# A hybrid encoder layer: the squares of W1 and of the input rows taken by ScalarE's accumulator instead of GpSimd sums

## The chip, the cores and the metric

One NeuronCore of a Trainium2 chip runs the whole layer in one launch. The metric is the device time of one execution in microseconds (us), lower is better. The engines are TensorE (PE; PEld is its weight load), VectorE (DVE), ScalarE (ACT), GpSimd (POOL) and SyncE (SP), which here issues every DMA of the kernel, in program order.

## The reference, cut to what matters

Input x has 2048 tokens of width 1024, all float32; there is one layer.

```python
h = rms_norm(x, norm1_g)
q, k, v, gb, gc, hin, u = split(h @ w_in)      # 3 x 512, then 4 x 256
q, k = rms_norm(q, q_norm_g), rms_norm(k, k_norm_g)          # 8 heads of 64
y_attn = chunked_band_attention(q, k, v, rel_bias)  # chunks of 64, own + 8 before
y_conv = gb * conv3(gc * hin, conv_w)
y_pool = (mean over the last 2, 4, 8, 16 tokens - u) @ pool_w * pool_scale
x = x + concat(y_attn, y_conv, y_pool) @ w_out
h2 = rms_norm(x, norm2_g)
x = x + square(relu(h2 @ w_mlp1)) @ w_mlp2     # 1024 -> 4096 -> 1024
```

The layer needs the mean square of every row of x for the first norm. The kernel's MLP runs in 16-bit halves, so it also needs a bound on the size of each column of `w_mlp1` (and of `w_mlp2`), from which it takes the powers of two that scale the operands. Finding these bounds is called the survey; it reads both weights once (64 tiles of 128x512 each) beside the attention part.

## The kernel before

Tokens are worked on in four blocks of 512 (`block(b, ...)`). Activations are held column-major: a tile of x has 128 model columns as partitions and 512 tokens along the free axis. Each block has these stages, and the order of TensorE's instructions over all of them is fixed by hand (`weave` takes attention units and fills in side work at a set rate, `InOrder` chains TensorE's instructions). The other engines and SP follow the scheduler's priorities, and each executes its own queue in order.

- **Projection.** `project(0)`, `project(1)` and `project(2)` make q, k and v, each in 8 steps over the model columns. A step loads a weight tile `rwq` (`load_w`, L137 to L143), ACT rounds it to the high part (L141), DVE subtracts to get the low part (L142), and TensorE runs 12 matmuls (three products of high and low parts for four groups of 128 tokens, L160 to L162). `project(0)` also loads the x tile (`load_x`, L392): ACT makes its high part (L395), DVE its low part (L396).
- **Row powers of x.** In `load_x` the helper `sumsq` (L203) squares the x tile on ACT and adds the square to `acc` on POOL (L209). After the eighth step `token_cols` (L211) sums `acc` over partitions with TensorE against a column of ones, in four float32 matmuls (L214) into a PSUM tile of tag "d", and DVE scales the sum (L216). `rsqrt` (an ACT square root and DVE steps) gives `rstd`. The same helpers serve the output rows (`acc2`, in `outproj`), which the change leaves alone.
- **Attention**, 32 units per block: scores (L529, L530), softmax (L533, L539), a transpose of the probabilities (L550) that ACT and DVE write as high and low part `pp` (L551, L552), values (L565). `prep` transposes k and q for the next two heads, and spreads them through DRAM and by DMA (`kd`, `kx`, `qs`, `qx`).
- **Side work**, woven between the units: the output projection of the block before (`outproj`, with `xo`, which is read, added to and stored to `x2d`), conv and pooling (`convpool`), the second norm's statistics (`stats`), and the survey.
- **Survey.** `pace` asks for one step of `survey` in two of five steps of side work. For W1 a step loads two tiles `pr` (tag "x", five buffers shared with the x tiles), ACT squares each to bfloat16 (L283), POOL adds them in three pieces (L286 to L288) into a group tile, and after eight steps TensorE sums over partitions with eight one-column matmuls (L271) that DVE copies out. For W2 a step loads two tiles `ps`, and ACT squares each with its accumulator (L300), which leaves one sum per partition. `paced` ties each square behind the latest softmax exponential on ACT.
- **Early operands.** In block 3 `early_operands` prepares the MLP input of the first tokens: it loads `er` and `e` tiles, scales them on DVE (L358), and `put` (L364, L365) writes 28 pairs of 16-bit halves, two buffers of tag "pg", each stored to DRAM (`xd`, L366).
- **MLP**, from 896 us on: Strassen-like products in 16-bit halves (L845), with all operands already scaled.

Of the kernel before, what the change touches and what calls it, by code (L numbers as in the profile page):

```python
# [8 lines left out]
F32 = mybir.dt.float32  # L9
# [9 lines left out]
P = 128  # L19
D = 1024  # L20
# [72 lines left out]
def trunk(ctx, tc, xT, cols, cinv, w_qkv, w_cp, w_out, w1, w2, nbias, pool_w, outT):  # L93
# [32 lines left out]
    ones16 = const.tile([P, 1], BF16, name="ones16")  # L126
    ve.memset(ones16, 1.0)
# [98 lines left out]
    vacc = p1.tile([P, 512], F32, name="vacc")  # L226
# [11 lines left out]
    def value_norms(k):  # L238
        raw = scr.tile([P, 512], F32, tag="x", bufs=5, name=f"vw{k}")
# [18 lines left out]
    cn = const.tile([P, FF // P], F32, name="cn")  # L258
# [8 lines left out]
    def survey():  # L267
        def norms(f0, group):
            t = pd(f"cn{f0}")
            for i in range(8):  # L270
                te.matmul(t[:, i : i + 1], group[:, i], ones16, start=True, stop=True)  # L271
            ve.tensor_copy(cn[:, f0 : f0 + 8], t[:, 0:8])

        full = None
        for ft in range(FF // P):
            if ft % 8 == 0:
                group = scr.tile([P, 8, P], BF16, tag="pg", bufs=2, name=f"pg{ft}")
            qs = []
            for half in range(2):
                raw = scr.tile([P, 512], F32, tag="x", bufs=5, name=f"pr{ft}_{half}")  # L280
                sy.dma_start(raw, w1[ft, half])
                q = scr.tile([P, 4, P], BF16, tag="pq", bufs=3, name=f"pq{ft}_{half}")
                paced(sc.activation(q.rearrange("p a b -> p (a b)"), raw, AF.Square))  # L283
                qs.append(q)
            q = qs[0]
# [3 lines left out]
            if ft % 8 == 2 and full:  # L289
                norms(*full)  # L290
            if ft % 8 == 7:
                full = (ft - 7, group)
            yield
        yield
        norms(*full)
        for i in range(64):
            raw = scr.tile([P, 512], F32, tag="x", bufs=5, name=f"ps{i}")
            sy.dma_start(raw, w2[i // 16, (i // 2) % 8, i % 2])
            q = scr.tile([P, 512], BF16, tag="pq", bufs=3, name=f"pt{i}")
            paced(sc.activation(q, raw, AF.Square, accum_out=sq2[:, i : i + 1]))  # L300
            if i % 2:
                yield

# [21 lines left out]
    def scales():  # L325
        for _ in surveyed:
            pass
        m = const.tile([P, 4], F32, name="m")
        ve.tensor_reduce(out=m[:, 0:1], in_=cn, axis=AX.X, op=ALU.max)
# [18 lines left out]
    def early_operands():  # L348
        for k in range(4):
            q = {}  # L350
            for n in range(2):
                rr = scr.tile([P, 512], F32, tag="x", bufs=5, name=f"er{k}_{n}")
                sy.dma_start(rr, r2d[n])
                for half in range(2):
                    kk = k + 4 * half
# [725 lines left out]
```

## Time and profile before

| | us |
| --- | --- |
| median of 3 runs | 2143.21 (2143.02 to 2146.45) |
| the profiled execution | 2144.97 |
| span of its trace | 2143.1 |

| engine | busy | share of the span |
| --- | --- | --- |
| TensorE | 2050.1 us | 96% |
| VectorE | 1365.9 us | 64% |
| ScalarE | 1010.9 us | 47% |
| GpSimd | 700.1 us | 33% |

The clock granted to TensorE was 0.986 of full speed on average. DMA moved 392.88 MB. A busy share is an average over stages; an idle stretch of TensorE shows in the view of waits with the engine and tile that ended it. A row of the timeline gives start, duration, engine, line, operation, tiles, and in brackets the idle time just ahead and what ended it.

### The profile page before, as it was taken

How to read it: one execution, taken by the hardware profiler on the slowest of the kernel's cores; microseconds unless marked ns; L12 is line 12 of the kernel's file. 1: busy time of each engine (PE TensorE's matmuls, PEld its weight loads, DVE VectorE, ACT ScalarE, POOL GpSimd, SP SyncE). 2: the span in 40 equal slices, each digit the busy share in tenths (PEclk: the TensorE clock that was granted, in tenths of full speed). 3: DMA queues.
4: the chain of work that ended last, by engine and by line, in shares of the span. 5: the costliest groups of instructions: out<-in, count | busy, mean ns of one | idle time of the engine just before them, and what ended most of it. 6: DMA issues, size and time to landing. Idle time of an engine off the chain costs nothing.

```text
span 2143.1 us, 31845 instructions
## 1 busy us (share of the span) xinstructions
PE 2050.1 (96%) x11136; PEld 1262.3 (59%) x11136; DVE 1365.9 (64%) x2184; ACT 1010.9 (47%) x1940; POOL 700.1 (33%) x565
## 2 busy tenths in 40 slices
PE   7999998999899699998999999999999999999999
PEld 6777787888787588864444444444444444444444
DVE  7687466856679767757768878767743053353354
ACT  5466465737665455545656446446134151150330
POOL 4254055200224213154546456445522031130132
PEclk9999999999999899999999999999999999999999
DMA  8685698549866776493465565547743333333344
GB/s 287 202 242 169 173 273 248 179 121 273 266 199 211 241 225 179 136 344 116 161 221 189 174 209 182 182 148 286 259 120 102 104 101 101 103 97 106 103 148 152
DMA packets 215824, 392.88 MB, mean 183 GB/s; under 512 B 25584, under 2 KB 32880, under 8 KB 215664
## 3 DMA queue, kind: packets, MB, share of 16 engines
q1 hardware_dynamic: 215664, 390.86, 58.2%
q8 instruction: 87, 1.43, 0.3%
q14 instruction: 73, 0.60, 0.1%
HBM read 268.60 MB, written 105.38 MB: 175 GB/s over the span
## 4 chain that ended last, share of the span: by engine, by line
PE 68%; DMA 10%; DVE 9%; issue 5%; POOL 4%; ACT 3%; SPq 1%; POOLq 0%; DVEq 0%; ACTq 0%
PE b_d L845 21%; PE b_u L845 18%; PE a L161 3%; PE a L162 3%; PE a L160 3%; PE cp L160 2%; PE o L160 2%; PE cp L161 2%; PE cp L162 2%; PE o L161 2%; PE o L162 2%; PE pt L550 2%; PE y L565 2%; DMA r_d<-w 1%; PE s L529 1%
## 5 line engine op out<-in xcount | busy, mean ns | idle before, releaser
L845 PE MATMUL b_d<-ft_u,s_d 128*128 128x512 f16 x1152 | 265.8, 381 | 7.6 <-ACT ft_u L795 3.2
L845 PEld LDWEIGHTS <-s_d 128*128 128x128 f16 x1536 | 150.5, 98 | 191.3 <-issue 10.6
L845 PEld LDWEIGHTS <-s_u 128*128 128x128 f16 x1536 | 150.6, 98 | 186.5 <-issue 7.2
L845 PE MATMUL b_u<-zt,s_u 128*128 128x512 f16 x1152 | 257.3, 381 | 1.5 <-DVE u2u L948 0.8
L966 DVE TENSOR_TENSOR acc<-acc,b_d 128x512 f32<-128x512 f32 x176 | 119.1, 682 | 179.7 <-PE b_d L845 175.4
L845 PEld LDWEIGHTS <-a_u 128*128 128x128 f16 x1152 | 112.8, 98 | 146.6 <-issue 13.5
L845 PEld LDWEIGHTS <-a_d 128*128 128x128 f16 x1152 | 112.8, 98 | 143.2 <-issue 8.4
L829 POOL TENSOR_TENSOR t1u<-u2u,c11u 128x512 f32<-128x512 f32 x32 | 43.6, 1363 | 443.5 <-ACT u2u L952 431.3
L845 PE MATMUL b_d<-fb_u,a_d 128*128 128x512 f16 x768 | 183.7, 379 | 4.0 <-DVE acc L966 1.7
L845 PE MATMUL b_u<-zb,a_u 128*128 128x512 f16 x768 | 176.6, 379 | 1.3 <-ACT u2u L935 1.3
L209 POOL TENSOR_TENSOR acc<-acc,sq 128x512 f32<-128x512 f32 x56 | 82.8, 1479 | 260.4 <-ACT sq L208 191.3
L161 PE MATMUL a<-wq,xg 128*128 128x512 f32 x384 | 155.3, 404 | 8.2 <-DVE wq L142 8.2
L160 PE MATMUL a<-wq,xg 128*128 128x512 f32 x384 | 147.4, 407 | 10.4 <-ACT wq L141 7.8
L162 PE MATMUL a<-wq,xg 128*128 128x512 f32 x384 | 154.5, 403 | 0.1
L539 ACT ACTIVATE sb<-sb,nm 128x640 f32<-128x640 f32 (+4 forms) x128 | 97.6, 762 | 115.8 <-DVE nm L533 111.5
L552 DVE SCALAR_TENSOR_TENSOR pp<-pt,pp 128x384 f16<-128x384 f32 (+1 forms) x224 | 101.8, 483 | 48.2 <-ACT pp L551 47.6
L533 DVE CUSTOM_DVE_ANT_0 sb<-s,b 128x640 f32<-128x640 f32 (+4 forms) x128 | 94.1, 735 | 52.7 <-PE s L530 51.3
L142 DVE TENSOR_TENSOR wq<-rwq,wq 128x512 fp32r<-128x512 f32 x96 | 79.9, 839 | 46.0 <-ACT wq L141 46.0
L160 PE MATMUL o<-mix,wo 128*128 128x512 f32 x256 | 106.3, 416 | 1.3 <-ACT mix L631 1.0
L160 PE MATMUL cp<-xg,wc 128*128 128x512 f32 x256 | 107.1, 418 | 0.0
L141 POOL CAST wc<-rwc 128x512 fp32r<-128x512 f32 x64 | 41.8, 653 | 195.4 <-PE cp L162 94.2
L935 ACT COPY u2u<-b_u 128x512 f32<-128x512 f32 x32 | 18.5, 578 | 179.8 <-PE b_u L845 177.5
(274 smaller groups left out, 4512.1 us busy)
## 6 DMA issues: line engine op xcount, KB each, us to landing
rwq<-w_qkv SPq DMA_DIRECT2D x96, 256.0 KB, 2.8
pr<-w SPq DMA_DIRECT2D x64, 256.0 KB, 4.8
rwc<-w_cp SPq DMA_DIRECT2D x64, 256.0 KB, 4.3
rwo<-w_out SPq DMA_DIRECT2D x64, 256.0 KB, 4.4
ps<-w SPq DMA_DIRECT2D x64, 256.0 KB, 4.5
r_u<-w SPq DMA_DIRECT2D x64, 256.0 KB, 3.4
wd<-s_u SPq DMA_DIRECT2D x64, 256.0 KB, 2.2
r_d<-w SPq DMA_DIRECT2D x64, 256.0 KB, 2.9
```

Source lines behind the costliest of these rows:

```text
L142: (lo or ve).tensor_tensor(out=w[:, 1], in0=raw, in1=w[:, 0].bitcast(F32), op=ALU.subtract)
L160: te.matmul(out, ah, bh, start=start, stop=False)
L161: te.matmul(out, ah, bl, start=False, stop=False)
L162: te.matmul(out, al, bh, start=False, stop=stop)
L209: gp.tensor_tensor(out=acc, in0=acc, in1=q, op=ALU.add)
L533: ve.tensor_tensor_reduce(out=sb[:, :nk].rearrange("p (e k) -> p e k", e=ne), in0=s[:, :ne, :hk], in1=bi[:, 640 - nk :].rearrange("p (e k) ...
L539: exps.append(sc.activation(sb[:, :nk], sb[:, :nk], AF.Exp, bias=nmx, scale=-1.0, accum_out=st["l"][:, i, j : j + 1]))
L550: te.transpose(pt[:, m * P : (m + 1) * P], sb[:, c0 + m * P : c0 + (m + 1) * P], ident)
L552: ve.scalar_tensor_tensor(out=pp[:, 1, c0:c1], in0=pt[:, :n], scalar=PSC, in1=pp[:, 0, c0:c1], op0=ALU.mult, op1=ALU.subtract)
L829: gp.tensor_tensor(out=t1, in0=b12, in1=b11, op=ALU.subtract)
L845: te.matmul(bank, w[:, a, q * P : (q + 1) * P], xs[q][:, c], start=start and q == 0 and i == 0, stop=q == n - 1 and i == 2, skip_group_che ...
L966: ve.tensor_tensor(out=a, in0=a, in1=bk, op=ALU.add)
```

## The change

- **Survey of W1.** The kernel gets a second input, `w1t`, which is W1 stored with its columns along the partitions (the host lays it out). All 128 squares of the survey are now in one loop: ACT's square with `accum_out` leaves one sum per partition, in `sq1` for W1 and `sq2` for W2. A step loads two tiles (tag "sv", four buffers) and squares the two tiles of the step before. The POOL adds, the one-column matmuls, the DVE copies and the "pq" tiles go; one DVE reduction of `sq1` is added in `scales`.
- **Row powers of x.** A third input, `xN`, is x in token-major tiles. Each step of `project(0)` also loads an `xn` tile (tag "sv"), and two steps later ACT squares it with the accumulator into `sx`. DVE reduces `sx` (`row_stats`). The POOL adds and the matmuls of this sum go; the 32 added loads are 8.4 MB.
- **Early operands.** `er` is loaded twice in all, not eight times (1.5 MB less), the four `e` tiles of a step come in one go (tag "sv"), and are worked on a step later.
- **Buffers.** Tag "x" has three buffers, not five; "sv" has four; `vacc` shares the tag "acc".

```diff
@@ sumsq, value_norms
-            q = pool.tile([P, TB + 16], F32, tag="win", bufs=2, name="sq")[:, :TB] if pool is scr else pool.tile([P, 512], F32, tag="sq", bufs=1, name="sq")
+            q = pool.tile([P, 512], F32, tag="sq", bufs=1, name="sq")
-    vacc = p1.tile([P, 512], F32, name="vacc")
+    vacc = p1.tile([P, 512], F32, tag="acc", name="vacc")
@@ survey
-            for half in range(2):
-                raw = scr.tile([P, 512], F32, tag="x", bufs=5, name=f"pr{ft}_{half}")
-                sy.dma_start(raw, w1[ft, half])
-                q = scr.tile([P, 4, P], BF16, tag="pq", bufs=3, name=f"pq{ft}_{half}")
-                paced(sc.activation(q.rearrange("p a b -> p (a b)"), raw, AF.Square))
...
-            gp.tensor_tensor(out=q, in0=q, in1=qs[1], op=ALU.add)
-            gp.tensor_tensor(out=q[:, :2], in0=q[:, :2], in1=q[:, 2:], op=ALU.add)
-            gp.tensor_tensor(out=group[:, ft % 8], in0=q[:, 0], in1=q[:, 1], op=ALU.add)
...
+        srcs = [w1t[i // 2, i % 2] for i in range(64)] + [w2[i // 16, (i // 2) % 8, i % 2] for i in range(64)]
+        held = []
+
+        def look():
+            i, raw = held.pop(0)
+            acc = (sq1, sq2)[i // 64][:, i % 64 : i % 64 + 1]
+            paced(sc.activation(raw, raw, AF.Square, accum_out=acc))
+
+        for i, src in enumerate(srcs):
+            raw = scr.tile([P, 512], F32, tag="sv", bufs=4, name=f"{'prt'[2 * (i // 64)]}{i}")
+            sy.dma_start(raw, src)
+            held.append((i, raw))
             if i % 2:
+                while len(held) > 2:
+                    look()
                 yield
@@ scales
+        ve.tensor_reduce(out=cn, in_=sq1.rearrange("p (f t) -> p f t", t=2), axis=AX.X, op=ALU.add)
@@ early_operands
-                rr = scr.tile([P, 512], F32, tag="x", bufs=5, name=f"er{k}_{n}")
-                sy.dma_start(rr, r2d[n])
...
+            for half in range(2):
+                for n in range(2):
+                    raw[half, n] = scr.tile([P, 512], F32, tag="sv", bufs=4, name=f"e{k}_{half}{n}")
+                    sy.dma_start(raw[half, n], x2d[k + 4 * half, :, n * 512 : n * 512 + 512])
+            yield
@@ block
-            xr = scr.tile([P, 512], F32, tag="x", bufs=5, name=f"x{b}_{k}")
+            xr = scr.tile([P, 512], F32, tag="x", bufs=3, name=f"x{b}_{k}")
-            sumsq(acc, xr, k == 0, scr)
+        def row_power(n):
+            raw = scr.tile([P, 512], F32, tag="sv", bufs=4, name=f"xn{b}_{n}")
+            sy.dma_start(raw, xN[4 * b + n // 2, n % 2])
+            return n, raw
+
+        def look_rows(n, raw):
+            sc.activation(raw, raw, AF.Square, accum_out=sx[:, n // 2, n % 2 : n % 2 + 1])
...
+                if c == 0:
+                    rows.append(row_power(k))
+                    if k > 1:
+                        look_rows(*rows.pop(0))
...
-        ms1 = token_cols(acc, f"ms1_{b}")
-        rstd = rsqrt(sm, ms1, NT, "r1")
+            ve.tensor_reduce(out=ms1, in_=sx, axis=AX.X, op=ALU.add)
+            ve.tensor_scalar(ms1, ms1, 1.0 / D, EPS, op0=ALU.mult, op1=ALU.add)
+            rstd.append(rsqrt(sm, ms1, NT, "r1"))
```

Three places of the instruction order follow, before and after.

Place one, block 1 with the statistics of block 0. SP's queue, from the store of `xo0_6` to the next survey loads (`pr28_1` is a tile of W1), before:

```order
L732 DMA x2d_102<-xo0_6_3902 128x512
L730 DMA xo1_0_5955<-xT 128x512
L139 DMA rwc1_0_0_4218<-w_cp 128x512
L475 DMA qs1_5_3762<-qlo1_2_3685 64x512
L470 DMA kx1_5_3760<-kd_105 128x1024
L475 DMA qs1_5_3762<-qhi1_2_3684 64x512
L475 DMA qx1_5_3763<-qhi1_2_3684 64x512
L475 DMA qx1_5_3763<-qlo1_2_3685 64x512
L481 DMA b1_5_3770<-bd_104 128x640
L281 DMA pr28_1_4188<-w1 128x512
```
The same queue after (`p54` and `p55` are tiles of `w1t`):

```order
L742 DMA x2d_100<-xo0_6_3740 128x512
L740 DMA xo1_0_5729<-xT 128x512
L137 DMA rwc1_0_0_4031<-w_cp 128x512
L485 DMA qs1_5_3611<-qlo1_2_3534 64x512
L480 DMA kx1_5_3609<-kd_103 128x1024
L485 DMA qs1_5_3611<-qhi1_2_3533 64x512
L485 DMA qx1_5_3612<-qhi1_2_3533 64x512
L485 DMA qx1_5_3612<-qlo1_2_3534 64x512
L491 DMA b1_5_3619<-bd_102 128x640
L276 DMA p54_3874<-w1t 128x512
L276 DMA p55_3876<-w1t 128x512
```
One survey load stood behind `b1_5` before, the second of its pair being issued earlier; now both loads of a pair, `p54` and `p55`, stand there. ACT's queue at the same place, before:

```order
L539 ACTIVATE sb1_4_1_4122,l1_2_4062<-sb1_4_1_4122,nm1_4_1_4123 128x640
L283 ACTIVATE pq28_0_4186<-pr28_0_4184 128x512
L283 ACTIVATE pq28_1_4190<-pr28_1_4188 128x512
L551 ACTIVATE pp1_4_0_4137<-pt1_4_0_0_4138 128x384
L551 ACTIVATE pp1_4_0_4137<-pt1_4_0_384_4144 128x256
L166 ACT_TABLE_LOAD
```
and after:

```order
L549 ACTIVATE sb1_4_1_3940,l1_2_3880<-sb1_4_1_3940,nm1_4_1_3941 128x640
L272 ACTIVATE p54_3874,sq1_116<-p54_3874 128x512
L272 ACTIVATE p55_3876,sq1_116<-p55_3876 128x512
L561 ACTIVATE pp1_4_0_3955<-pt1_4_0_0_3956 128x384
L561 ACTIVATE pp1_4_0_3955<-pt1_4_0_384_3962 128x256
L164 ACT_TABLE_LOAD
```
The two squares stand at the same place as before, between the exponential of unit 4_1 and the write of `pp1_4_0`; the table load for the square root is still behind them.

Place two, the first projection of block 0, on DVE (`xg` is the low part of x, `wq` that of the weight, `bi` a bias table), before:

```order
L142 TENSOR_TENSOR wq0_0_2_193<-rwq0_0_2_191,wq0_0_2_193 128x512
L396 SCALAR_TENSOR_TENSOR xg0_3_128<-x0_3_208,col_92,xg0_3_128 128x512
L199 TENSOR_SCALAR bi0_346<-nb0_349,col_92 128x256
L200 MEMSET bi0_346 64x64
L396 SCALAR_TENSOR_TENSOR xg0_4_129<-x0_4_232,col_92,xg0_4_129 128x512
L396 SCALAR_TENSOR_TENSOR xg0_5_130<-x0_5_256,col_92,xg0_5_130 128x512
L199 TENSOR_SCALAR bi1_354<-nb1_357,col_92 128x256
L142 TENSOR_TENSOR wq0_0_3_217<-rwq0_0_3_215,wq0_0_3_217 128x512
L200 MEMSET bi1_354 64x64
L396 SCALAR_TENSOR_TENSOR xg0_6_131<-x0_6_280,col_92,xg0_6_131 128x512
L142 TENSOR_TENSOR wq0_0_4_241<-rwq0_0_4_239,wq0_0_4_241 128x512
```
and after:

```order
L140 TENSOR_TENSOR wq0_0_2_191<-rwq0_0_2_189,wq0_0_2_191 128x512
L384 SCALAR_TENSOR_TENSOR xg0_3_126<-x0_3_206,col_92,xg0_3_126 128x512
L140 TENSOR_TENSOR wq0_0_3_215<-rwq0_0_3_213,wq0_0_3_215 128x512
L384 SCALAR_TENSOR_TENSOR xg0_4_127<-x0_4_230,col_92,xg0_4_127 128x512
L197 TENSOR_SCALAR bi0_342<-nb0_345,col_92 128x256
L140 TENSOR_TENSOR wq0_0_4_239<-rwq0_0_4_237,wq0_0_4_239 128x512
```
Before, `xg0_4`, `xg0_5` and a bias piece stood between `xg0_3` and `wq0_0_3`; now each weight follows its x tile at once.

Place three, block 3, on ACT: from the square root of k's norms (`rqs` of `ssk3`) to the high part of k (`khi3_0`), with the casts of `put` (`eb` and `et`, 28 in all) between, before:

```order
L166 ACTIVATE rqs_8558<-ssk3_8541 128x32
L141 CAST wq3_2_5_8655<-rwq3_2_5_8653 128x512
L364 CAST eb22_2_10861<-e2_11_10792 128x512
L141 CAST wq3_2_6_8681<-rwq3_2_6_8679 128x512
L364 CAST et1_2_10872<-e2_00_10687 128x512
L364 CAST et3_2_10876<-e2_01_10748 128x512
L141 CAST wq3_2_7_8722<-rwq3_2_7_8720 128x512
L364 CAST et2_2_10919<-e2_11_10792 128x512
L141 CAST wo2_0_1_8759<-rwo2_0_1_8757 128x512
L364 CAST et4_2_10923<-e2_10_10723 128x512
L141 CAST wo2_0_0_8764<-rwo2_0_0_8762 128x512
L452 CAST khi3_0_8628<-tk3_0_8623 128x512
```
and after:

```order
L353 CAST et1_2_10524<-e2_00_10332 128x512
L164 ACTIVATE rqs_8280<-ssk3_8263 128x32
L139 CAST wq3_2_6_8403<-rwq3_2_6_8401 128x512
L353 CAST et3_2_10528<-e2_01_10334 128x512
L353 CAST et2_2_10549<-e2_11_10338 128x512
L139 CAST wq3_2_7_8444<-rwq3_2_7_8442 128x512
L353 CAST et4_2_10553<-e2_10_10336 128x512
L139 CAST wo2_0_1_8481<-rwo2_0_1_8479 128x512
L353 CAST eb11_3_10653<-e3_00_10597 128x512
L139 CAST wo2_0_0_8486<-rwo2_0_0_8484 128x512
L462 CAST khi3_0_8350<-tk3_0_8345 128x512
L353 CAST eb21_3_10679<-e3_10_10601 128x512
```
`rqs` stood after `eb21_2`, and now stands two puts later, after `et1_2`; `khi3_0` stood after `et4_2`, and now stands one put later, after `eb11_3`.

## Rows read from the trace of the kernel before

**Rows 1.** The page: busy time, share of the span, instructions, by engine.

```profile
PE 2050.1 (96%) x11136; PEld 1262.3 (59%) x11136; DVE 1365.9 (64%) x2184; ACT 1010.9 (47%) x1940; POOL 700.1 (33%) x565
```

**Rows 2.** View of waits, TensorE, 0 to 900 us: total us, times, longest us.

```profile
PE s L529 <- DMA qx<-qlo: 13.0, 1, 13.0
PE a L161 <- DVE wq L142: 8.2, 6, 3.2
PE tq L448 <- DVE klo L453: 4.2, 2, 3.8
PE y L565 <- DVE pp L552: 3.8, 4, 2.2
PE tq L448 <- DVE r1r L173: 3.3, 1, 3.3
PE s L529 <- DVE nm L533: 2.3, 2, 1.7
PE a L160 <- DVE ms_3c L216: 2.3, 1, 2.3
```

**Rows 3.** Busy us by stretch: length, PE, PEld, DVE, ACT, POOL, clock, DMA share, GB/s.

```profile
411.00:431.00 20.00, 17.34 (x96) 13.85 (x95) 18.75 (x20) 14.03 (x28) 10.86 (x7) 0.91 0.67 201
...
900.00:2143.00 1243.00, 1212.04 (x5570) 561.47 (x5568) 725.89 (x894) 494.86 (x826) 444.87 (x303) 1.00 0.50 163
```

**Rows 4.** Timeline, block 0, first projection: start us, us, engine, line, operation, tiles.

```profile
7.77 0.69 DVE L142 TENSOR_TENSOR wq<-rwq,wq 128x512 fp32r<-128x512 f32 x1 [0.41 <-ACT wq L141]
12.56 1.78 DVE L142 TENSOR_TENSOR wq<-rwq,wq 128x512 fp32r<-128x512 f32 x1
...
17.48 3.33 DVE L396 SCALAR_TENSOR_TENSOR xg<-x,col,xg 128x512 fp32r<-128x512 f32 x2
21.73 0.79 PE L161 MATMUL a<-wq,xg 128*128 128x512 f32 x1 [3.16 <-DVE wq L142]
22.75 0.63 PE L160 MATMUL a<-wq,xg 128*128 128x512 f32 x1
```

**Rows 5.** DMA view, 4 to 15 us.

```profile
DMA packets 2218, 3.64 MB, mean 331 GB/s; under 512 B 247, under 2 KB 631, under 8 KB 2218
```

**Rows 6.** Timeline of TensorE: a sum over partitions, and matmuls behind it.

```profile
332.69 1.03 PE L214 MATMUL ms<-ones,acc 128*128 128x1 f32 x8
...
333.90 0.39 PE L161 MATMUL cp<-xg,wc 128*128 128x512 f32 x1
334.13 0.39 PE L162 MATMUL cp<-xg,wc 128*128 128x512 f32 x1
```

**Rows 7.** Timeline of DVE and POOL, block 0, attention.

```profile
130.70 2.48 DVE L653 SCALAR_TENSOR_TENSOR m<-w,uh 64x512 f32<-64x512 f32 x2
131.07 1.57 POOL L286 TENSOR_TENSOR pq<-pq,pq 128x512 bf16<-128x512 bf16 x1
```

**Rows 8.** Timeline of TensorE, first projection of block 2.

```profile
419.27 0.50 PE L161 MATMUL a<-wq,xg 128*128 128x512 f32 x1 [2.66 <-DVE wq L142]
```

**Rows 9.** Groups by form, ACT, 0 to 900 us: busy us, mean ns.

```profile
L300 ACT ACTIVATION_READ_ACCUMULATOR pt<-ps 128x1 f32 x64 | 12.1, 188 | 0.0
```

**Rows 10.** Timeline of SP, block 1, around place one.

```profile
322.85 0.38 SPq L732 DMA_DIRECT2D x2d<-xo  x1
327.81 0.33 SPq L730 DMA_DIRECT2D xo<-xT  x1
```

**Rows 11.** Timeline of ACT, then of TensorE, block 1, behind place one.

```profile
339.54 0.63 ACT L283 ACTIVATE pq<-pr 128x512 bf16<-128x512 f32 x1 [6.54 <-DMA pr<-w]
...
341.19 0.77 PE L550 MATMUL pt<-ident,sb 128*128 128x128 f32 x5 [3.55 <-DVE pp L552]
```

**Rows 12.** Timeline of ACT, block 3: puts, and the root of k's norms.

```profile
662.85 0.62 ACT L364 CAST eb<-e 128x512 f16<-128x512 f32 x1 [1.62 <-DVE e L358]
...
709.53 0.23 ACT L166 ACTIVATE rqs<-ssk 128x32 f32<-128x32 f32 x1
...
723.79 0.62 ACT L364 CAST et<-e 128x512 f16<-128x512 f32 x1 [3.21 <-DMA xd<-et]
```

More of the change, by code (lines that the diff above doesn't have):

```diff
@@ L238, in value_norms @@
     def value_norms(k):
-        raw = scr.tile([P, 512], F32, tag="x", bufs=5, name=f"vw{k}")
+        raw = scr.tile([P, 512], F32, tag="x", bufs=3, name=f"vw{k}")
         sy.dma_start(raw, w_qkv[2, k])
@@ L256, in value_scale @@
         ve.tensor_scalar(vsc[:, 1:2], r, 1.0 / (1024.0 * PSC), None, op0=ALU.mult)
-    cn = const.tile([P, FF // P], F32, name="cn")
+    sq1 = const.tile([P, 64], F32, name="sq1")
     sq2 = const.tile([P, 64], F32, name="sq2")
@@ L267, in survey @@
     def survey():
[L268 to L278, printed above, removed]
-            for half in range(2):
-                raw = scr.tile([P, 512], F32, tag="x", bufs=5, name=f"pr{ft}_{half}")
-                sy.dma_start(raw, w1[ft, half])
-                q = scr.tile([P, 4, P], BF16, tag="pq", bufs=3, name=f"pq{ft}_{half}")
-                paced(sc.activation(q.rearrange("p a b -> p (a b)"), raw, AF.Square))
-                qs.append(q)
-            q = qs[0]
-            gp.tensor_tensor(out=q, in0=q, in1=qs[1], op=ALU.add)
-            gp.tensor_tensor(out=q[:, :2], in0=q[:, :2], in1=q[:, 2:], op=ALU.add)
-            gp.tensor_tensor(out=group[:, ft % 8], in0=q[:, 0], in1=q[:, 1], op=ALU.add)
[L289 to L300, printed above, removed]
+        srcs = [w1t[i // 2, i % 2] for i in range(64)] + [w2[i // 16, (i // 2) % 8, i % 2] for i in range(64)]
[8 more added lines that the diff above has]
+            held.append((i, raw))
             if i % 2:
+                while len(held) > 2:
+                    look()
                 yield
+        while held:
+            look()
     surveyed = survey()
@@ L348, in early_operands @@
     def early_operands():
-        for k in range(4):
-            q = {}
-            for n in range(2):
-                rr = scr.tile([P, 512], F32, tag="x", bufs=5, name=f"er{k}_{n}")
-                sy.dma_start(rr, r2d[n])
-                for half in range(2):
-                    kk = k + 4 * half
-                    t = scr.tile([P, 512], F32, tag="x", bufs=5, name=f"e{k}_{half}{n}")
-                    sy.dma_start(t, x2d[kk, :, n * 512 : n * 512 + 512])
-                    ve.scalar_tensor_tensor(out=t, in0=t, scalar=g2s[:, kk : kk + 1], in1=rr, op0=ALU.mult, op1=ALU.mult)
+        rr = []
+        for n in range(2):
+            t = scr.tile([P, 512], F32, tag="x", bufs=3, name=f"er{n}")
+            sy.dma_start(t, r2d[n])
+            rr.append(t)
+        for k in range(4):
+            raw, q = {}, {}
+            for half in range(2):
+                for n in range(2):
+                    raw[half, n] = scr.tile([P, 512], F32, tag="sv", bufs=4, name=f"e{k}_{half}{n}")
+                    sy.dma_start(raw[half, n], x2d[k + 4 * half, :, n * 512 : n * 512 + 512])
+            yield
+            for half in range(2):
+                for n in range(2):
+                    kk, t = k + 4 * half, raw[half, n]
+                    ve.scalar_tensor_tensor(out=t, in0=t, scalar=g2s[:, kk : kk + 1], in1=rr[n], op0=ALU.mult, op1=ALU.mult)
                     q[half, n] = t
-                    yield
+                yield
             def put(src, op):
@@ L407, in project @@
                 ac = [pd(f"a{b}_{c}_{i}", "dydt"[i]) for i in range(4)]
+            rows = []
             for k in range(KT):
```

22 lines of the change are left out of this document (14 added, 8 removed).

## The prediction

> **What bounds the kernel now.** I read the page's busy shares first, then the waits of TensorE, then the stretches, and last the timelines around each long wait. TensorE is busy 96% of the span, GpSimd 33% [rows 1]. The only time to be won is TensorE's own work and its waits. From 900 us on it is busy 1212 of 1243 us [rows 3], its instructions there are the same in both kernels, and nothing of the change reaches there: I count that part as 0. So everything happens in the attention part, and there the waits that bear on the change are few [rows 2]: one wait of 13.0 us for `qx` in block 3, six waits for the low part of a weight (8.2 us), and 15.9 us in the other five lines, all of which name DVE and none GpSimd. GpSimd is not a bound. It can matter only through DVE: a low part `wq` takes 0.69 us alone at 7.77, and 1.78 us at 12.56, where a POOL add runs [rows 4]; in block 0's attention two DVE steps take 2.48 us beside the survey's add of 1.57 us [rows 7].
>
> The page "SBUF — State Buffer" of the Trainium skill (section "Who interferes with whom") states a rule for this: a DVE instruction with two SBUF inputs shares a port with a GpSimd instruction that reads SBUF, and the later one is held for the whole of the other. The trace agrees, 0.69 against 1.78 us. By the rule alone DVE could be given back up to the POOL time that goes, and the sum would be that of the second rival below.
>
> **The change part by part.** The profiled execution took 2144.97 us, 1.9 us above its span and 1.8 above the median of 2143.21. I sum against 2145.0.
>
> *Start of block 0.* DVE works on `xg0_4` and `xg0_5` ahead of the weight that TensorE needs (3.33 us for two, [rows 4]), and TensorE waits 3.16 us. In the new order (place two) the weight follows its x tile at once and no POOL add is beside it: this wait goes. Behind it TensorE runs at the lower level of its clock for a while, 0.63 us for a matmul [rows 4]. What this costs I take from the like wait in block 2, 2.66 us [rows 8], in a stretch of 20 us with a granted clock of 0.91 [rows 3]: 20 x 0.09 = 1.8 us, part of it idle anyway, so 1.5. Against it, one 256 KB tile `xn0_0` now comes ahead of the first weight: at 331 GB/s [rows 5] a tile takes 0.79 us, so +0.8. Term: -3.2 - 1.5 + 0.8 = **-3.9** (-4.7 to 0, if another wait takes its place).
>
> *TensorE's own work.* A sum over partitions is 4 float32 matmuls, recorded as 8. From 332.69 to 333.90 stand these eight and one matmul of 0.23 us (the distance of the next two), so 0.98 us at most [rows 6]; I take 0.9. The input's four go: 3.6 us. The 32 one-column bfloat16 matmuls of the survey are not more than 0.98 / 8 = 0.12 us each by that row (3.9 us), and not below 0. They have operands of half the width, so I take 0.8, nearer the lower end. Of the 4.4 us, 0.9 stand in block 3 ahead of the long wait and are counted there. Term: **-3.5** (-6.9, with 0.98 and 0.12, to -2.7).
>
> *Block 0's attention.* With no survey adds beside it, DVE's two-input steps fall back toward 0.7 us. The waits there are those for the score minimum `nm` (2.3) and some of those for `pp` (3.8) [rows 2]: 6.1 in all. I take half, since the chain TensorE-DVE-ACT-TensorE stays. Term: **-3** (-6 to 0).
>
> *First projections of blocks 1 to 3.* Of the 8.2 us for `wq`, 3.2 are at the start and 2.7 in block 2; the other 2.3 lie in four short waits. Here DVE loses the contention of eight POOL adds, but ACT, in order, has more to do: each accumulated square adds a read of 188 ns [rows 9], 96 of them, 18.0 us over the kernel, while the count of squares is unchanged. In block 2 the last `pp` writes of the block before stand behind two of the new squares, so the low part is only some 1.5 us earlier. I take -1.2 for the short waits, -1.7 for block 2 and +0.7 for block 3, where the squares of `xn3_5` to `xn3_7` come ahead of the casts. Term: **-2.2** (-6.5, all waits and the clock loss gone, to +3).
>
> *Place one, the statistics in blocks 1 and 2.* SP waits about 4.6 us (322.85 to 327.81) to issue the next load of `xo`, which needs the store to `x2d` [rows 10]. Everything behind it in its queue is late, the survey loads too. ACT then waits 6.54 us for a survey tile, and TensorE 3.55 us for `pp` [rows 11] and 3.3 us for the square root `r1r`, which ACT has behind the tile [rows 2]. "Loads a step ahead" sounds as if it ended this. The order says no: `p54` and `p55` are issued at the same place, behind the same nine DMAs, and their squares stand ahead of `pp1_4_0` as before. Now the second of two loads is waited for, which is a tile more (0.79 us) in each of the two blocks. Term: **+1.6** (-10.6, if 3.55, 3.3 and block 2's 3.8 for `klo` [rows 2] all go, to +3 for two more tiles in each).
>
> *Block 3.* The wait for `ms_3c` (2.3 us, [rows 2]) goes with its PSUM tile. The puts pace ACT: the first at 662.85, the 21st at 723.79 [rows 12], 60.94 / 20 = 3.05 us each. The `xn` squares end sooner than the old x squares did, so I start the puts about 3 us earlier. The root of k's norms ran at 709.53 behind put 16. Behind put 18 it comes at 662.85 - 3 + 17 x 3.05 + 0.6 = 712.3, 2.8 us later. The high part of k, now behind put 22, comes at 662.85 - 3 + 21 x 3.05 + 0.6 = 724.5, about where it was. So the 13.0 us for `qx` stay, and swallow part of what was won ahead of them. Term: **-2**, with the 0.9 of the sum over partitions in it (-4 to +6, two puts late and nothing won).
>
> *Copies, reductions and buffers.* The removed DVE copies and the new reductions are a few short DVE instructions far from TensorE's chain: 0. Net DMA traffic grows by 6.8 of 393 MB, at 331 GB/s 21 us of transfer, mostly in first projections; that is covered by TensorE's work there unless the first rival below holds.
>
> Sum: -3.9 - 3.5 - 3 - 2.2 + 1.6 - 2 = -13.0. 2145.0 - 13.0 = 2132.0 for an execution like the profiled one, and 1.8 less, **2130 us**, for the median.
>
> **The rivals.**
>
> 1. *The loads of `xn` bind (slower).* A step of `project(0)` has now three loads, 3 x 0.79 = 2.4 us at the rate of the start [rows 5], against 12 matmuls of 0.23 us [rows 6], 2.8 us. In block 2 that stretch already moves 201 GB/s at a share of 0.67 [rows 3]. Eight tiles more in 22 us are 95 GB/s more, a share of 0.67 x 296 / 201 = 0.99. From there each step waits, as SP's and ACT's queues are in order. Price if every added tile is paid: 32 x 0.79 = 25 us, 2155. For it: that share. Against it: three x tiles of the next block are now loaded a block ahead, and survey loads pause there. Chance 0.16.
>
> The page "DMA: Bandwidth & Descriptors" of the Trainium skill (section "Queues, rings and completion order") states that all DMAs that SP issues go through one row of rings and are taken in ring order, so an added tile holds up every later weight. No row here separates that from plain saturation; it speaks for this rival.
>
> 2. *DVE and the statistics gain fully (faster still).* All DVE waits outside block 3's long one shorten, and the loads a step ahead do end ACT's waits at place one. Then place one gives -10.6 and not +1.6 (2118), with the other terms as they are. For it: every one of these waits names DVE or ACT work that the change lightens. Against it: place one's order. Chance 0.15.
>
> 3. *No change to speak of: the change does not do what it says for TensorE.* The DVE waits of block 0 and of the first projections come from the chain of dependences, not from POOL, and block 3 pays a put. Left are start, own work and place one, -5.8, and +2 of block 3: 2145.0 - 3.8 - 1.8 = 2139. For it: the `pp` waits hang on ACT's cast too. Against it: the stretched steps [rows 4, 7]. Chance 0.15.
>
> **How the numbers follow.** The forecast (2122 to 2138) has 0.54, the rivals 0.16, 0.15 and 0.15. A measurement of this kernel can tell about 0.2% from no change, 4.3 us, so 2138.9 is the edge. Faster: 0.54 + 0.15 and 0.03 of the third rival, 0.72. Slower: nearly all of the first, 0.15. Same: 0.13. The range goes from 2115, a little below the second rival, to 2147, which takes in the third and leaves out most of the first.
>
> **What would show it.** In the trace after: no wait of TensorE near 18 us, and a first matmul at about 8.5; no POOL instruction between block 0's projections and its output sums but the value norms and the pooling windows; low parts of about 0.7 us in first projections; ACT still waiting 6 to 8 us for `p54` or `p55` near 330 and for `t106` near 565; the wait for `qx` still 10 to 15 us. The forecast is wrong if first projections show TensorE waiting for `rwq` or ACT for `xn` (first rival), or if ACT's wait at place one is gone (second).

## The result

The changed kernel takes 2132.47 us (median of four runs, 2131.75 to 2134.14), the kernel before 2143.11 us beside it; the ratio is 0.995, with a 95% interval of 0.9933 to 0.9967. Timed again in five rounds it was 0.9944 (0.9926 to 0.9962). The forecast was 2130 us, in a range of 2115 to 2147. The size is right; several of its terms are not, and that they cancel is luck.

TensorE's busy time fell by 10.1 us, GpSimd's by 121 us. The page's busy line, after, answers to [rows 1]:

```profile
PE 2040.0 (96%) x11072; PEld 1255.2 (59%) x11072; DVE 1339.8 (63%) x2184; ACT 1019.6 (48%) x2036; POOL 579.0 (27%) x441
```
TensorE's waits of the attention part, after (total us, times, longest us; the lines that bear on the change), answer to [rows 2]:

```profile
PE s L539 <- DMA qs<-qlo: 14.9, 2, 12.7
PE a L158 <- ACT wq L139: 12.5, 3, 8.4
PE tq L458 <- DVE klo L463: 10.0, 4, 3.8
PE y L575 <- DVE pp L562: 7.8, 6, 1.6
PE pt L560 <- DVE pp L562: 7.3, 8, 2.2
PE a L159 <- DVE wq L140: 1.8, 1, 1.8
PE tk L458 <- DVE nk L445: 1.7, 1, 1.7
PE s L539 <- DVE nm L543: 0.8, 1, 0.8
```
One line of the same view of before is not in [rows 2]:

```profile
PE pt L550 <- DVE pp L552: 5.8, 3, 3.5
```
The six waits for a low part `wq` are down from 8.2 to 1.8 us, those for `nm` from 2.3 to 0.8, and the wait for `ms_3c` is gone. The wait for `r1r` has only changed its name: the same matmul, at 345.85 us before and 337.68 after, now waits 3.77 us for `klo`. New is ACT's `wq`: of its 12.5 us, 8.4 are the start of the first matmul (7.8 before), and 4.1 are two waits for a high part at changes of block. `pp` costs 15.1 us in 14 waits, where it was 9.6 in seven. The wait of block 3 is 12.7 us, where it was 13.0.

One profile is not enough to place 10 us here. Both kernels were profiled again, and I compare the start of the same TensorE matmul in each profile with its start in the first profile of before (positive: earlier, in us):

```
matmul at, in the first profile    before,   changed kernel   steps
of before                          2nd       1st  2nd  3rd    moved
block 0, end of projection   84     0.0      4.4  4.6  3.7     4.8
block 0, attention          160    -0.4      5.2  5.1  3.8     5.4
block 1, projection done    235     0.1      4.0  6.2  1.6     5.0
block 1, attention begun    257     0.7      7.3  7.0  3.1     6.1
block 1, before its stats   331     0.7      6.9  6.2  1.3     0.9
block 1, behind its stats   350     1.2      7.5  6.1  1.3     8.9
block 2, projection done    475     2.8     11.0  9.3  4.8    10.2
block 2, before its stats   566     3.6      8.2  9.9  4.4     5.2
block 2, late               640     4.9      7.4 11.9  3.6    11.5
block 3, projection 0       654     4.9      4.3 10.0  0.9     9.1
block 3, end                896     4.1      8.0 14.5  4.1    13.3
MLP                        2100     3.7     13.1 15.2  7.1    15.9
```

(The third profile of the changed kernel is that of experiment 9, `steps moved` that of experiment 10.) The attention part of one and the same kernel ends 4 us apart in two profiles of before, and 10 us apart in three of the changed kernel. On average over the profiles the changed kernel leads before by 6.8 us at 896 us and by 10.0 at 2100: about 7 us come from the attention part, where the forecast had 13, and 3 from the MLP, where it had 0. The MLP, whose instructions are the same, gave -0.4 in the second profile of before and +5.1, +0.7 and +3.0 in those of the changed kernel. The 5.1 us of the first are mostly one wait near 1041 us and what follows it: 2.17 us in the first profile of before, 1.81 in the second, 0.74 in the first of the changed kernel, with matmuls at the lower clock behind it only in the first (nine take 3.79 us, and 2.10 in the others). TensorE's timeline, the first profile of before, then its second, then the changed kernel:

```profile
1041.66 3.79 PE L845 MATMUL b_d<-ft_u,s_d 128*128 128x512 f16 x9 [2.17 <-ACT ft_u L795]
```
```profile
1037.27 2.10 PE L845 MATMUL b_d<-ft_u,s_d 128*128 128x512 f16 x9 [1.81 <-ACT ft_u L795]
```
```profile
1031.94 2.10 PE L855 MATMUL b_d<-ft_u,s_d 128*128 128x512 f16 x9 [0.74 <-ACT ft_u L805]
```
The lower clock is the first profile's of before alone. The shorter wait is not scatter: it is 0.5 to 1.0 us in all twelve profiles of kernels with the change or a part of it, and 1.8 or more in both of before. ACT waits there for POOL, and POOL for a weight tile `r_d` (4.50 and 4.17 us in the two profiles of before, 2.98 in the first of the changed kernel). Why that tile lands sooner is open; it is worth about 1 us. The rest of the MLP I count as scatter, and judge what follows by medians of timed runs first, and by the traces where a mechanism is to be seen.

### The profile page after: what moved, and what is told of

Same layout as the page of the kernel before. It is cut to its first block, busy times and chain, and to the rows that moved or that the text cites. A ratio compares the mean times of both kernels' runs of the same rounds, so it can differ in the third digit from the quotient of the medians.

```text
span 2130.1 us, 31726 instructions
## 1 busy us (share of the span) xinstructions
PE 2040.0 (96%) x11072; PEld 1255.2 (59%) x11072; DVE 1339.8 (63%) x2184; ACT 1019.6 (48%) x2036; POOL 579.0 (27%) x441
## 4 chain that ended last, share of the span: by engine, by line
PE 38%; DVE 5%; POOL 3%; DMA 3%; issue 3%; ACT 2%; SPq 0%; POOLq 0%; DVEq 0%; ACTq 0%
PE b_d L855 21%; PE b_u L855 17%; DMA r_d<-w 1%; DVE ft_u L806 1%; POOL t1u L839 1%; DVE a_d L809 1%; DVE acc L976 1%; DVE s_d L809 1%; POOL r_d L824 0%; DVE x L869 0%; POOL s_d L822 0%; DVE a_u L809 0%; DMA rr<-r2d 0%; DMA xd<-yb 0%; ACT ft_u L805 0%
## 5 line engine op out<-in xcount | busy, mean ns | idle before, releaser
L855 PEld LDWEIGHTS <-a_u 128*128 128x128 f16 x1152 | 112.7, 98 | 146.3 <-issue 12.7
L158 PE MATMUL a<-wq,xg 128*128 128x512 f32 x384 | 144.6, 403 | 12.5 <-ACT wq L139 12.5
L207 POOL TENSOR_TENSOR acc<-acc,sq 128x512 f32<-128x512 f32 x28 | 38.0, 1357 | 379.2 <-ACT sq L206 353.0
L158 PE MATMUL cp<-xg,wc 128*128 128x512 f32 x256 | 106.7, 417 | 0.0
L159 PE MATMUL cp<-xg,wc 128*128 128x512 f32 x256 | 101.5, 397 | 0.0
```

Of the source, the lines that this page charges most:

```text
L158: te.matmul(out, ah, bh, start=start, stop=False)
L159: te.matmul(out, ah, bl, start=False, stop=False)
L855: te.matmul(bank, w[:, a, q * P : (q + 1) * P], xs[q][:, c], start=start and q == 0 and i == 0, stop=q == n - 1 and i == 2, skip_group_che ...
```

## The experiments

Ratios are to the kernel before, timed on the same chip, with their 95% intervals; the changed kernel has 0.995 and 0.9944.

**1. The survey alone.** The row powers of x as before:

```diff
+            sumsq(acc, xr, k == 0, scr)        # in load_x, with its POOL adds
-                    rows.append(row_power(k))
+        ms1 = token_cols(acc, f"ms1_{b}")
```

> The change with the row powers of x taken as before (squares of the x tiles on ACT, sums on POOL, four float32 matmuls), the survey and the early operands as changed; no tiles of x are loaded twice. Theory (the rows of x give most at the start and in TensorE's own work, and lose at the first projections of blocks 1 and 3, where ACT meets the new squares in its queue): TensorE waits near 18 us for the low part of a weight again, no wait for the first weight of blocks 1 and 3; 2136 to 2141 us. Rival (nearly all of the gain is the survey's, through fewer POOL adds): 2131 to 2134 us, with the waits of block 0's attention shorter than before by 3 us or more.

Measured: 2137.22 us, 0.9969 (0.9953 to 0.9986), so the time is as the theory had it. One of its signs came true: TensorE's wait for the first weight is 0.39 us in block 1 and under 0.2 in block 3, where the changed kernel has 2.04 and 2.06. The other did not: there is no wait near 18 us, and the 49th matmul of the first projection starts 4.8 us earlier than in before, with the POOL adds of the row powers in place. What this kernel shares there with the changed one, and with that of experiment 2, is the order on DVE: one x tile, then its weight. That the order does it is read from this; it was not tried alone.

**2. The row powers alone.** The kernel before with `xN`, no POOL adds and no matmuls for the sum:

```diff
-            sumsq(acc, xr, k == 0, scr)
+            raw = scr.tile([P, 512], F32, tag="x", bufs=6, name=f"xn{b}_{n}")
+            sc.activation(raw, raw, AF.Square, accum_out=sx[:, n // 2, n % 2 : n % 2 + 1])
```

> The kernel before with only the row powers of x changed (token-major tiles, accumulated squares); survey and early operands as before, the added tiles share tag x, which has six buffers. Theory: the wait near 18 us is gone (-3), the sums over partitions are gone (-3.6), and the first projections lose 2 to 5 us to ACT's queue: 2137 to 2141 us. Rival (the survey gives nearly all): 2142 to 2144 us. Rival (the rows give nearly all): 2131 to 2135 us.

Measured: 2132.11 us, 0.9945 (0.9926 to 0.9964), the time of the whole change: the second rival. The start's gain is in both halves (3.9 us at the 49th matmul here), so they don't add up, and the new survey on top of the new row powers gives nothing that can be measured. The profile shows a second reason: this kernel, with the old survey, has a gain at place one that the changed kernel lacks. Its queue holds the survey loads ahead of the wait for `x2d`:

```profile
329.79 1.00 SPq L281 DMA_DIRECT2D pr<-w  x2
330.96 0.33 SPq L754 DMA_DIRECT2D x2d<-xo  x1
...
335.74 0.33 SPq L752 DMA_DIRECT2D xo<-xT  x1
```
ACT waits for no survey tile there, and from 331 to 350 us (before's time) 7.5 us are won. Whether the sixth buffer of tag x does this or another order of the queue, no run separates.

**3. POOL adds put back.** 28 two-input adds whose result nothing uses:

```diff
+            if k:
+                gp.tensor_tensor(out=junk, in0=xg[:, 0].bitcast(F32), in1=xg[:, 0].bitcast(F32), op=ALU.add)
```

> The changed kernel with 28 POOL adds of two inputs put back into the first projections; they read the high part of x and write a tile that nothing uses, so nothing waits for their result. Theory (POOL's adds stretch DVE, and the gain at the start is partly theirs): low parts of 1.4 to 1.8 us beside the adds instead of 0.7, TensorE waits 1 to 3 us more in the first projections, 2133 to 2137 us. Rival (the start's gain is the order alone, weights before later x tiles): low parts may be longer, the time stays within 1 us of the changed kernel, 2131.5 to 2133.5 us.

Measured: 2139.87 us, 0.9979 (0.9967 to 0.999), some 6 to 7 us above the changed kernel; the theory's direction, and more than its 1 to 5. The DVE groups of the x tiles' low parts (line, busy us, mean ns), in this kernel and in the changed one:

```profile
L386 DVE SCALAR_TENSOR_TENSOR xg<-x,col,xg 128x512 fp32r<-128x512 f32 x32 | 33.4, 1050 | 5.3 <-ACT xg L385 5.2
```
```profile
L384 DVE SCALAR_TENSOR_TENSOR xg<-x,col,xg 128x512 fp32r<-128x512 f32 x32 | 23.7, 749 | 8.9 <-ACT xg L383 8.6
```
In the trace nothing waits for the added instructions. The price does not fall at the start: its projection ends 4.2 us ahead of before's, as in the changed kernel (4.4). In this profile the price falls in the first projections of blocks 2 and 3 (0.7 us lost from 350 to 475 us where the changed kernel wins over 3, and 4.5 lost from 640 to 654 where the changed kernel loses 1.9 to 3.1), where DVE also has the last attention units. TensorE in block 2, with the adds back:

```profile
411.47 0.50 PE L159 MATMUL a<-wq,xg 128*128 128x512 f32 x1 [1.00 <-DVE wq L140]
...
415.38 0.20 PE L579 MATMUL y<-vp,pp 128*128 128x64 f16 x1 [2.41 <-DVE pp L566]
```
The profiled run is 5 us above the median of its ten. As far as this one trace shows, a change of block where DVE is the late one pays for POOL, and the start, where DVE has time to spare, does not.

**4. Loads of `xN` without their squares.** In blocks 1 to 3 six of eight squares left out:

```diff
-            sc.activation(raw, raw, AF.Square, accum_out=...)
+            if n > 5 or b == 0:
+                sc.activation(raw, raw, AF.Square, accum_out=...)
```

> The changed kernel, in blocks 1 to 3 with six of the eight squares of token-major x tiles left out (their loads stay, the sums are set to 512, so the norm is not the reference's there). Theory (the first projections of blocks 1 and 3 lose because ACT, in order, has squares and their waits ahead of the casts and of the last pp): the waits there shrink by 4 to 5 us in all, 2126 to 2129 us. Rival (they lose because eight more loads delay the weights): the waits stay, 2131 to 2133 us.

Measured: 2132.09 us, 0.9942 (0.9923 to 0.9962): the changed kernel's time. The rival's time, but not its mechanism in block 1. In the changed kernel ACT waits there 1.33 us for a tile `xn` that stands ahead of the first weight's cast. ACT, then TensorE:

```profile
174.97 0.63 ACT L394 ACTIVATE xn<-xn 128x512 f32<-128x512 f32 x1 [1.33 <-DMA xn<-xN]
...
175.60 0.60 ACT L139 CAST wq<-rwq 128x512 fp32r<-128x512 f32 x1
```
```profile
173.75 0.47 PE L575 MATMUL y<-v,pp 128*128 128x64 f16 x10 [1.05 <-DVE pp L562]
...
176.25 0.50 PE L158 MATMUL a<-wq,xg 128*128 128x512 f32 x1 [2.04 <-ACT wq L139]
```
Without the squares TensorE's wait is 0.69 us and not 2.04:

```profile
173.39 0.50 PE L158 MATMUL a<-wq,xg 128*128 128x512 f32 x1 [0.69 <-ACT wq L139]
```
At 235 us this kernel is 6.2 us ahead of before, the changed kernel 4.0, 6.2 and 1.6. What block 1 gains is not seen in the end: in block 3 the wait for the weight is 0.55 us and not 2.06, but a wait of 2.21 us for `pp` stands ahead of it instead, and at 896 us the lead is 8.4. The squares are one of several things that end last at a change of block.

**5 and 6. Both kernels again**, to size the scatter.

> The kernel before, unchanged, profiled a second time. Theory (5 of the 13 us between the two profiles are in the MLP and are chance): the attention part, to 896 us, ends within 1.5 us of the first profile, and the MLP behind it is 2 to 5 us shorter. Rival (the change makes the MLP faster): the MLP is as long as in the first profile within 1 us, with the wait of 2.2 us near 1041 us.

> The changed kernel, unchanged, profiled a second time. Theory: the attention part ends within 1.5 us of the first profile (888 us), the MLP differs from the first by up to 4 us either way. Rival: both parts repeat within 1 us.

Measured: 2141.31 and 2129.78 us. The attention parts ended 4.1 and 6.4 us earlier than in the first profiles, so the theories of 1.5 us failed. Before's MLP was 0.4 us longer than in its first profile, not 2 to 5 shorter, as the rival had it; the changed kernel's MLP differed by 4.4 us from its first, a little more than the theory's 4. That before's MLP repeats in length is chance: its second profile lacks the 1.7 us of lower clock near 1041 us and loses 2.6 between 1500 and 1600. So of the 5.1 us of the first profiles 1.7 are that lower clock of before, 1.4 the shorter wait there, and the rest is scatter. Where its attention part differs is place one of block 2: ACT waited 2.30 us for the survey tile in the second profile, 5.07 in the first.

**7. Two survey steps left out near the statistics of blocks 1 and 2.**

```diff
-                if n % 5 < 2:
+                if n % 5 < 2 and not (b in (1, 2) and n in (31, 36)):
```

> The changed kernel with two survey steps left out near the statistics of blocks 1 and 2 (they come at the end of the survey instead), so that no square of a tile loaded behind the wait for x2d stands ahead of the last pp. Theory (ACT's waits of 4.8 and 5.1 us for survey tiles hold up pp and the square root): these waits go, and TensorE gets back 3 to 6 us by 600 us. Rival (the pp and the square root wait as long for their own chain, DVE and the table loads): TensorE's waits there stay within 1 us of the changed kernel.

Measured: 2130.11 us, 0.9918 (0.9889 to 0.9947). The theory: ACT's waits of 4.83 and 5.07 us are gone, and TensorE passes from 331 to 350 us with 7 us won. The survey now ends in block 3, and the early operands come behind it: no cast of `put` stands ahead of `khi3_0`, where 22 do in the changed kernel. TensorE's waits in block 3, from 640 us on:

```profile
PE rb L220 <- DVE r1r L171: 7.1, 1, 7.1
...
PE s L539 <- DMA qs<-qlo: 4.2, 1, 4.2
```
The long wait falls from 12.7 to 4.2 us, which bears out the forecast's reading that the puts set it; at 745 us this profile is 37 us ahead of before. By 896 us 26 of them are lost to waits beside the late casts, the new one of 7.1 us among them. The profiled run is the slowest of five, 8.5 us above their median.

**8. The row powers in the second projection.**

```diff
-                if c == 0:
+                if c == 1:
                     rows.append(row_power(k))
```

> The changed kernel with the token-major x tiles loaded and squared in the second projection of each block, not the first, and the statistics behind it. Theory (the squares and their loads cost 2 to 3 us at the change of block, in blocks 1 and 3): TensorE's waits at 165 to 180 us and at 645 to 655 us shrink by 4 to 5 us in all, 2127 to 2130 us. Rival (what is won there is lost again at the start of the attention units, where the transfers of q and k end last): 2131 to 2133 us.

Measured: 2141.67 us, 0.9972 (0.9955 to 0.9988): by the ratios 5 to 6 us above the changed kernel, against both. In block 0 the second projection already loads a `vw` tile in each step. With `xn` a step has three, and bias tables besides. ACT waits for weights, then TensorE:

```profile
44.90 0.62 ACT L139 CAST wq<-rwq 128x512 fp32r<-128x512 f32 x1 [1.94 <-DMA rwq<-w_qkv]
...
50.97 0.62 ACT L139 CAST wq<-rwq 128x512 fp32r<-128x512 f32 x1 [1.25 <-DMA rwq<-w_qkv]
...
53.04 0.62 ACT L139 CAST wq<-rwq 128x512 fp32r<-128x512 f32 x1 [1.45 <-DMA rwq<-w_qkv]
```
```profile
48.28 0.79 PE L159 MATMUL a<-wq,xg 128*128 128x512 f32 x1 [2.83 <-DVE wq L140]
```
This is the first rival of the forecast, in a place where I had not looked: 5.9 us are lost from the 145th to the 169th matmul, 2.8 of them the wait and most of the rest matmuls at the lower level of the clock (0.72 granted from 44 to 56 us, 1.00 in the changed kernel).

**9. The changed kernel once more, and 10, the two steps moved, not dropped.**

```diff
-                if n % 5 < 2:
+                if n % 5 < 2 and not (b in (1, 2) and n in (31, 36)) or b in (1, 2) and n in (3, 8):
```

> The changed kernel, unchanged, timed again beside the two kernels that build on it. Both theories: 0.993 to 0.997 of the kernel before.

> As the kernel with two survey steps left out near the statistics of blocks 1 and 2, but the two steps are done earlier in the same block, so that the survey ends where it ended. Theory (the squares of tiles loaded behind the wait for x2d cost TensorE 3 to 6 us): 3 to 6 us below the changed kernel, and no survey work in block 3. Rival (what is won is lost again at the next waits, the change of block and the long wait of block 3): within 1.5 us of the changed kernel.

Measured, beside each other: 2133.96 us, 0.9944 (0.9926 to 0.9962), and **2129.04 us, 0.9919 (0.9901 to 0.9937)**, 4.9 us between them, as the theory had it. This is the fastest kernel with the survey where it was. The changed kernel at place one, block 1, first ACT, then TensorE, answers to [rows 11]:

```profile
330.30 0.63 ACT L272 ACTIVATE p<-p 128x512 f32<-128x512 f32 x1 [4.83 <-DMA p<-w1t]
...
332.35 1.28 ACT L164 ACT_TABLE_LOAD   x1
```
```profile
332.70 0.77 PE L560 MATMUL pt<-ident,sb 128*128 128x128 f32 x5 [1.93 <-DVE pp L562]
...
337.68 1.09 PE L458 MATMUL tq<-ident,nq 128*128 128x128 f32 x4 [3.77 <-DVE klo L463]
```
and in the kernel with moved steps the same two matmuls in block 1, and the second of them in block 2:

```profile
336.60 0.71 PE L560 MATMUL pt<-ident,sb 128*128 128x128 f32 x5
...
337.75 0.63 PE L458 MATMUL tq<-ident,nq 128*128 128x128 f32 x4
...
570.36 0.63 PE L458 MATMUL tq<-ident,nq 128*128 128x128 f32 x4 [0.94 <-DVE klo L463]
```
The squares there are of tiles loaded a step before the wait for `x2d`, and wait for nothing. From 331 to 350 us this kernel gains 8.0 us on before, the three profiles of the changed one 0.6, -0.1 and 0.0. In block 2, from 566 to 600 us, it gains 6.8, the three of the changed kernel -0.3, 2.5 and -0.3. But the moved steps cost something where they now stand. From 257 to 331 us this kernel loses 5.2 us and from 475 to 566 us 5.0; the changed kernel loses 0.4, 0.8 and 1.8 in the first stretch, and 2.8, -0.6 and 0.4 in the second. In block 1, ACT waits for survey tiles there, then TensorE for `pp`, and its next matmuls run at the lower level of the clock (0.72 granted from 281 to 287 us). ACT, then TensorE:

```profile
270.66 0.63 ACT L272 ACTIVATE p<-p 128x512 f32<-128x512 f32 x1 [1.39 <-DMA p<-w1t]
...
275.58 0.63 ACT L272 ACTIVATE p<-p 128x512 f32<-128x512 f32 x1 [3.54 <-DMA p<-w1t]
```
```profile
279.36 0.44 PE L560 MATMUL pt<-ident,sb 128*128 128x128 f32 x2 [1.64 <-DVE pp L562]
...
281.16 0.63 PE L158 MATMUL o<-mix,wo 128*128 128x512 f32 x1
```
So the 4.9 us are a net gain: more is won at place one, and part of it is paid elsewhere.

**11 and 12. The row powers of blocks 1 to 3 in the survey of the block before**, so that first projections have neither their squares nor their loads; at the old rate, and with six more steps in blocks 1 and 2:

```diff
+        srcs = ns(1) + ws[:28] + ns(2) + ws[28:80] + ns(3) + ws[80:]   # ns(b): eight tiles of xN
-                ... or b in (1, 2) and n in (3, 8):
+                ... or b in (1, 2) and n in (3, 8, 13, 18, 23, 43, 48, 53):
```

> On top of that, the row powers of blocks 1 to 3 are taken in the survey of the block before (eight tiles of token-major x per block go through its steps), so that the first projections of blocks 1 to 3 have no squares and no added loads. Theory (these squares and loads cost 2 to 5 us at the changes of block): 2 to 5 us below the one with moved steps alone. Rival (the changes of block are bound by other things, and the survey that now runs into block 3 costs as much): within 1.5 us of it, either way.

> The kernel with the row powers of blocks 1 to 3 in the survey of the block before, and six survey steps more in each of blocks 1 and 2, so that the survey ends at the end of block 2 as in the changed kernel. Theory (the survey that ran into block 3 cost its loss of 9 us there; without it the first projections are free of squares and added loads): 2125 to 2129 us, at or below the kernel with moved steps. Rival (the loss lies in the denser queues of ACT and the DMA, wherever the squares stand): 2131 us or more.

Measured: 2141.42 us, 0.9987 (0.997 to 1.0003), and 2133.02 us, 0.9952 (0.9938 to 0.9966). At the changes of block the theory holds: TensorE's wait for the first weight of blocks 1 and 3 is 0.29 and 0.39 us in the first kernel, 0.62 and none in the second, 2.04 and 2.06 in the changed one. The survey that runs into block 3 costs 7 to 8 us, which the second kernel has back. (In the first kernel the long wait of block 3 is 4.0 us, as in experiment 7, and 32 us are lost between 745 and 896 us.) Yet with the denser steps that one is slower than the kernel with moved steps, by 4 us in the medians and 7 by the ratios (0.9952 against 0.9919): the rival. Its profile loses 6.7 us from 257 to 331 us and 9.2 from 475 to 566, the stretches with the added steps. The work of the survey is not free beside attention; it is cheap at the rate it had.

## Why the prediction was right, and where its terms were off

- *The start* (-3.9, and 0.9 of own work): the projection of block 0 ends 4.4, 4.6 and 3.7 us earlier. Right in size, and the wait near 18 us is gone. The +0.8 for the tile ahead of the first weight is seen in two profiles of three: the first matmul is at 8.44, 7.70 and 8.47 us, in before at 7.79 and 7.47. The stretch of the start, after:

```profile
8.00:30.00 22.00, 21.56 (x83) 17.42 (x84) 14.11 (x34) 16.40 (x32) 0.00 (x0) 1.00 1.01 366
```
  The stretch moves 366 GB/s at a DMA share of 1.01 (after the clock, in the row), and TensorE is busy 21.56 of 22 us: the first rival's condition is met there, and its price is not paid. In block 2, for which the rival had estimated a share of 0.99, it is 0.92 at 310 GB/s (401 to 423 us). The sign that the forecast had named for this rival, ACT waiting for `xn`, did appear in the attention part:

```profile
ACT xn L394 <- DMA xn<-xN: 7.3, 8, 1.6
```
  Most of these waits are ACT's alone; one stands ahead of a weight's cast in block 1, and TensorE pays there (experiment 4). The reason given for the start was half wrong: experiments 1 and 3 show that the gain comes with the POOL adds there too, so it goes with the order, not with the missing adds.
- *TensorE's own work* (-4.4 in all): TensorE has 64 records less, and across the first sum over partitions, from the 85th to the 145th matmul, the lead grows by 0.6, 0.5 and 0.5 us, less than the 0.9 priced. The 32 one-column matmuls, priced at 0.8, were busy 1.4 us in before; no run separates what their removal is worth.
- *Block 0's attention* (-3): the step that failed. From 84 to 160 us the changed kernel gains 0.8, 0.5 and 0.1 us. The DVE steps are no longer stretched (the low parts `wc` take 710 ns there, 871 before; the steps `m` 681 and 952), and the waits for `nm` fell from 2.3 to 0.8 us, but those for `pp` rose from 3.1 us in two to 5.4 in four. I had priced the half of 6.1 us, of which 0.7 lay outside this stretch, and had taken the stretched DVE steps for what held these waits up. What holds `pp` up instead no experiment isolated.
- *First projections of blocks 1 to 3* (-2.2): right for block 2, where from 350 to 475 us it gains 3.2 to 3.5 us with the 0.9 of own work (before's second profile 1.6). Wrong for blocks 1 and 3. Block 1 loses 1.2 and 2.2 us in two of three profiles. Block 3 loses 1.9 to 3.1 us, where I had 0.7: in the first profile the row sum is ready so early that the table load of its root stands ahead of a weight's cast. ACT, then TensorE, after:

```profile
644.83 1.28 ACT L164 ACT_TABLE_LOAD   x1
646.13 0.20 ACT L164 ACTIVATE r1s<-ms 128x4 f32<-128x4 f32 x1
646.24 0.60 ACT L139 CAST wq<-rwq 128x512 fp32r<-128x512 f32 x1
```
```profile
646.89 0.49 PE L158 MATMUL a<-wq,xg 128*128 128x512 f32 x1 [2.06 <-ACT wq L139]
```
  That the root moves into the first projection stood in the order, and I had priced it at nothing. No run took the root alone away: without six of the squares most of this wait goes (experiment 4), and it goes without squares and loads (experiments 11 and 12).
- *Place one* (+1.6): the mechanism as forecast, both waits stay: ACT's for the survey tiles are 4.83 and 5.07 us, where they were 6.54 and 4.35. The forecast's 6 to 8 us, a tile more in each block, did not come. From 331 to 350 us 0.6 to -0.1 us are won, where before's second profile has 0.5, and from 566 to 600 us -0.3, 2.5 and -0.3, where it has 1.3: near 0. Experiments 7 and 10 show that the reading was right: the step ahead does nothing there, and moving two steps is worth, net, 5 of the 12 us that the forecast's second rival asked of both places.
- *Block 3* (-2): 3.7, 4.5 and 3.2 us won from 654 to 896, where before's second profile lost 0.8; the long wait stays, 12.7, 11.7 and 11.2 us. Experiments 7 and 11, with the puts behind it, bear out that they set it.
- *The start of attention in block 1*, counted at 0, gave 3.3, 0.8 and 1.5 us (235 to 257). *The MLP*, counted at 0 too, gave 5.1, 0.7 and 3.0: about 1 us is the shorter wait near 1041 us, which every kernel with the change or a part of it has; the rest comes and goes from profile to profile.
- *POOL.* The list of what would be left on it in block 0 lacked its casts of `wc`, of which 12 run from 84 to 160 us (13 before).

What the forecast took too much in block 0 (2.5 us) and at the changes to blocks 1 and 3 (about 2 each), it had too little in block 3, at the start of attention in block 1 and in the MLP, there mostly by chance. By the average of the profiles the attention part gave about half of what I had added up, so part of the hit is luck. What stays open is the size of every term of a few us, since the attention part of one kernel ends up to 10 us apart in three profiles.

The page "SBUF — State Buffer" of the Trainium skill ("Who interferes with whom") was borne out in kind by experiment 3: low parts of 1050 ns on average beside POOL's adds, 749 without, in the same kernel otherwise. The adds put back cost 6 to 7 us; by the one trace of that run they cost it where DVE is late.

The page "DMA: Bandwidth & Descriptors" of the Trainium skill ("Queues, rings and completion order") was cited for the first rival. In experiment 8 a third load per step did delay the weights; whether by ring order or by saturation no run separates.

## What to carry to other kernels

Before pricing a "load ahead", find in the issuing queue what the load stands behind: a step ahead in the program is no step ahead where both steps queue behind one wait, and moving the two steps away from it was worth, net of what they cost in their new place, nearly half of the whole change. After such a move, look at the new place too. Freeing an engine pays only where that engine ends last, so put the removed load back alone and see which stage pays. When a sum becomes ready earlier, ask what its consumers (here a table load) will now stand in front of.

## What the runs showed of the hardware that I had not expected

- The attention part of one kernel varied by up to 10 us from profile to profile, partly through the landing of single DMAs: the same survey tile kept ACT waiting 2.30 us in one profile and 5.07 in another.
- In the changed kernel a table load on ACT took 1.28 us, with 0.02 us idle ahead of it and 0.01 behind (at 644.83 us).
- Two halves of a change gave 0.9945 and 0.9969, and both together 0.995.
